# Time-mixing values kept once by token, the second direction read from them backwards, and a second raw-weight buffer in the first stage

## The chip, the cores and the metric

The kernel runs on one core of a Trainium2 chip. The metric is device time in microseconds (us) of one execution; the figure to compare is the median of several runs.

## The reference

One layer of a bidirectional hybrid backbone over 1024 latent tokens and 256 context tokens, 1024 channels, batch 1. A normalised and modulated input is projected by one matrix `w_in` into an S5 input, the RWKV-7 inputs (r, k, v and three low-rank columns) and gates. The two branches run side by side, are gated and merged, and a convolutional feed-forward follows. What matters here is the RWKV branch. It runs a delta rule over the tokens in both directions, 16 heads of 64 channels:

```python
def step(s, inp):
    rt, wt, kt, vt, at, bt = inp
    sa = jnp.einsum('bhvk,bhk->bhv', s, at)
    s = s * wt[:, :, None, :] + sa[..., None] * bt[:, :, None, :] + vt[..., None] * kt[:, :, None, :]
    return s, jnp.einsum('bhvk,bhk->bhv', s, rt)
...
ys_c, s_ctx = wkv7_scan(*ins_c, s_zero, rev)
ys_l, _ = wkv7_scan(*ins_l, s_ctx, rev)
```

Direction 1 reads the context tokens backwards and then the latent tokens backwards. The values v are the same for both directions.

## The kernel before

The program has three stages. **Stage A** (`stage_a`, from L600) normalises the input and runs the projections. Each projection job is a `dense` (L197): 8 x 3 matmuls a chunk of up to 512 tokens, since every weight is split into a high and a low part. `load_w` (L184) makes the two parts in two halves of 512 columns: SP issues the DMA of one half into the tile `wraw` (L191), ACT casts it to `whi` (L192), DVE subtracts to get `wlo` (L193). `wraw` has `E.nraw` buffers, and `E.nraw` is 1 through stage A (L1817) and 2 from stage C (L1858); `whi` and `wlo` have two buffers each. Around the projections the S5 branch runs in the same stage (`s5_in`, `s5_scan`, `s5_out`, lines 435 to 564), much of it on DVE and ACT; its loads (`s5bb`, `s5U`, `s5M`, `s5cc`) go through SP as well. The order in which the jobs of stage A are interleaved on the engines and on the queues is found by the framework's scheduler when the program is built, so jobs of the loop at L676 run between pieces of the S5 loop.

The loop at L676 has eight rounds j, one for each pair of heads (128 channels). It projects k, then v (`rw_job(16 + j)`, L678), then r. The v result `xs` is [128 channels, 1280 tokens]. It is stored as it is (L680), and also transposed: ten 128x128 transposes on TensorE into `pvt` (L687), three evictions by ACT into `vt` [128 tokens, 10, 128 channels] (L688), one store by POOL into the DRAM tensor `vT_d[j, 0]` by token (L689). Then SP issues two copies from DRAM to DRAM (L690 to L692): the rows of the 256 context tokens, and those of the 1024 latent tokens, each turned around, into `vT_d[j, 1]`. Both copies have the pattern "h t c": 2 heads outermost, then the tokens, then 64 channels (256 bytes) in one piece.

**Stage B** (`stage_b`, L1527) is the RWKV recurrence in 20 chunks of 64 tokens for each j, with both directions side by side, interleaved with the gate and GLU projections as filler work (`filler_nodes`). All of it is written as nodes of a `Plan` (L741). A node has an engine, a cost and dependencies; `order` (L761) is a list scheduler that puts all nodes into one order by due time, and PE, ACT and DVE run in that order. SP nodes ("s") cost 0.5 each in it. `chain_nodes` (L1160) holds the recurrence. Its helper `values` (L1173) loads the values of four chunks, both directions, into one of three tiles `V` [128, 2 directions, 4 chunks, 64]. Partitions 0 to 63 get the second head of the pair and 64 to 127 the first, through `OWN[1 - e]` at L1181. There are four loads, one for each direction and head, each of 256 tokens x 64 channels (64 KB) with the 64 tokens of a chunk on the partitions and outermost in the pattern. `values` is called five times for each j, 40 times in all, one block ahead of its use (L1215). The loads wait for the tile's earlier users (`gate`), and `B.a[d]` makes the chain wait for them.

**Stage C** (`stage_c`, L1647) has the output projections and the feed-forward. The change does not touch it.

SP issues its DMAs in order. The SP queue carries all weight loads, the S5 loads, the copies at L692, and in stage B the loads of every stage-B node.

Of the kernel before, what the change touches and what calls it, by code (L numbers as in the profile page):

```python
# [12 lines left out]
AF = mybir.ActivationFunctionType  # L13
# [6 lines left out]
CTX = 256  # L20
LAT = 1024
T = CTX + LAT
# [577 lines left out]
def stage_a(E):  # L600
    nc = E.nc
    with ExitStack() as st:
        spc = pool(E, st, "s5c", side="right")
        s_k = ExitStack()
        wp = stage_norm(E, st, spc, pool(E, s_k, "s5kc", side="right"))
        ps = E.ps
        rhs = lambda k, t0, n: (E.hh[:, k, t0:t0 + n], E.hl[:, k, t0:t0 + n])

        def u_load(U, g0):
            nc.sync.dma_start(U, E.u_d[g0 // 8, :, g0 % 8:g0 % 8 + 4, :])  # L610
        E.u_load = u_load

        def u_job(i):
            ut = wp.tile([128, 8, 160], FT, tag="raw", name="ut")

            def evac(pt, t0, n):
                nc.scalar.activation(ut[:, :, t0 // 8:(t0 + n) // 8], pt.rearrange("p (c s) -> p s c", s=8), AF.Copy)
            dense(E, wp, ps, E.I["win"][i], rhs, CH_ALL, evac, first=E.first if i == 0 else None)
            for g in range(8):
                nc.gpsimd.dma_start(E.u_d[i, :, g, :].rearrange("(s c) n -> c s n", c=16), ut[16 * g:16 * g + 16])  # L620

        def rw_job(m, chunks):
            raw = wp.tile([128, T], FT, tag="raw", name="raw")
            xs = wp.tile([128, T], FT, tag="xs", name="xs")

            def evac(pt, t0, n):
                nc.scalar.activation(raw[:, t0:t0 + n], pt, AF.Copy)
                nc.scalar.activation(xs[:, t0:t0 + n], pt, AF.Copy, scale=E.omu[:, m:m + 1])  # L628
            dense(E, wp, ps, E.I["win"][8 + m], rhs, chunks, evac)
            shift_lerp(E, m, raw, xs, chunks is CH_LAT)  # L630
            return xs

        def k_job(j):
            xs = rw_job(8 + j, CH_ALL)
            nc.gpsimd.dma_start(E.k_d[j], xs)
            kk = wp.tile([128, T], FT, tag="raw", name="kk")
            pk = ps.tile([128, 512], FT, tag="pz", name="pkk")
            for t0 in (0, 640):
                sq = kk[:, t0:t0 + 640]
                nc.scalar.activation(sq, xs[:, t0:t0 + 640], AF.Square, scale=E.par("kk", j))  # L640
                head_sums(E, pk[:, t0 // 64:], sq, 5)
            w = [wp.tile([128, 20], FT, tag=f"rs{i}", name=f"rs{i}", bufs=1) for i in range(3)]
            for f in rsqrt_small(E, w, lambda: pk[:, 0:20], None, None, 1e-24):
                f()

            def finish():
                for t0, n in CH_ALL:
                    pb = ps.tile([128, 512], FT, tag="pz", name="pkr")
                    head_spread(E, pb, w[1][:, t0 // 64:], n // 128)
                    nc.vector.scalar_tensor_tensor(kk[:, t0:t0 + n], xs[:, t0:t0 + n], E.par("kk", j), pb[:, :n],  # L650
                                                   op0=OP.mult, op1=OP.mult)
                nc.gpsimd.dma_start(E.kk_d[j], kk)
            return finish

        u_job(0)
        u_job(1)
        with ExitStack() as st2:
            s5_kernels(E, pool(E, st2, "s5k", 2, side="right"), ps)
        s_k.close()
        sp = pool(E, st, "s5p", side="right")  # L660
        S = s5_in(E, sp, ps, 0)
        for q in range(4):
            if q < 3:
                u_job(2 * q + 2)
                u_job(2 * q + 3)
                nxt = s5_in(E, sp, ps, q + 1)
            s5_scan(E, sp, S, q)
            s5_out(E, sp, ps, S, q)
            S = nxt
        xs = rw_job(24, CH_ALL)  # L670
        nc.scalar.activation(xs[0:64], xs[0:64], AF.Tanh)
        nc.gpsimd.dma_start(E.wda_d, xs)
        xs = rw_job(25, CH_LAT)
        nc.scalar.activation(xs[:, CTX:], xs[:, CTX:], AF.Sigmoid)
        nc.gpsimd.dma_start(E.gd_d, xs[:, CTX:])
        for j in range(8):  # L676
            finish = k_job(j)
            xs = rw_job(16 + j, CH_ALL)  # L678
            finish()
            nc.gpsimd.dma_start(E.v_d[j], xs)  # L680

            vt = wp.tile([128, 10, 128], FT, tag="raw", name="vt")
            for i in range(0, 10, 4):
                pv = ps.tile([128, 4, 128], FT, tag="pz", name="pvt")
                m = min(4, 10 - i)
                for q in range(m):
                    nc.tensor.transpose(pv[:, q, :], xs[:, 128 * (i + q):128 * (i + q) + 128], E.ident)  # L687
                nc.scalar.activation(vt[:, i:i + m], pv[:, 0:m], AF.Copy)  # L688
            nc.gpsimd.dma_start(E.vT_d[j, 0].rearrange("(i t) c -> t i c", t=128), vt)  # L689
            for c in (slice(0, CTX), slice(CTX, T)):  # L690
                src, dst = (E.vT_d[j, d, c].rearrange("t (h c) -> h t c", h=2) for d in range(2))
                nc.sync.dma_start(dst, src[:, ::-1])  # L692
            xs = rw_job(j, CH_LAT)
            nc.gpsimd.dma_start(E.r_d[j], xs[:, CTX:])

# [13 lines left out]
OWN = (slice(0, 64), slice(64, 128))  # L709
# [450 lines left out]
def chain_nodes(E, g):  # L1160


    nc, pl, j = E.nc, E.plan, g.j
# [7 lines left out]
    HALF = (0, 1)  # L1171

    def values(c0):  # L1173

        B, t0 = g.B[c0], 64 * c0
        sl, gate = E.V.next()
        B.V, B.Vslot = sl.tile, sl
        for d in HALF:
            for e in HALF:
                src = E.vT_d[j, d, t0:t0 + 256, 64 * e:64 * e + 64].rearrange("(i t) c -> t i c", t=64)  # L1180
                n = pl.add("s", 0.5, [gate], lambda d=d, e=e, src=src: nc.sync.dma_start(sl.tile[OWN[1 - e], d], src))  # L1181
                B.a[d].append(n)
                sl.users.append(n)

    def own(out, d, w, x, **kw):

# [621 lines left out]
def body(tc, I, O):  # L1808
    E = Env()
    E.tc, E.nc, E.I, E.O = tc, tc.nc, I, O  # L1810
    nc = tc.nc
    def ps_alloc(nb=None):
        E.ps = PsumPool(E, nb or {"d": 4})
    def ps_free():
        E.ps.st.close()
    E.ps_alloc, E.ps_free = ps_alloc, ps_free
    E.nraw = 1  # L1817
    with ExitStack() as st:
        E.const = pool(E, st, "const")
        E.dram = pool(E, st, "dram", 1, MS.DRAM)  # L1820
        dt = lambda n, s: E.dram.tile(s, FT, name=n, tag=n)
        E.u_d = dt("u_d", [8, 128, 8, 160])
        E.ge_d = dt("ge_d", [8, 128, LAT])
        E.r_d = dt("r_d", [8, 128, LAT])
        E.k_d = dt("k_d", [8, 128, T])
        E.kk_d = dt("kk_d", [8, 128, T])
        E.v_d = dt("v_d", [8, 128, T])
        E.sg_d = dt("sg_d", [16, 128, LAT])
        E.yg_d = dt("yg_d", [8, 128, LAT])
        E.y_d = dt("y_d", [8, 2, 128, LAT])  # L1830
        E.gd_d = dt("gd_d", [128, LAT])
        E.bon_d = dt("bon_d", [8, 2, 128, LAT])
        E.wda_d = dt("wda_d", [128, T])
        E.xn_d = dt("xn_d", [8, 128, LAT])
        E.vT_d = dt("vT_d", [8, 2, T, 128])
        E.inv_d = [[dt(f"{n}{k}", [64, 32, 32]) for n in ("LD", "TD", "AD")] for k in range(3)]
        E.acc_d = dt("acc_d", [8, 128, LAT])
        E.hx_d = dt("hx_d", [8, 128, LAT])
        constants(E)
        with ExitStack() as st1:  # L1840
            ps_alloc(NB_B)
            E.dtag = "sc"
            stage_a(E)
            with ExitStack() as st0:
                zero = pool(E, st0, "zero").tile([64, 256], FT, name="zero")
                nc.gpsimd.memset(zero, 0.0)
                for x in E.inv_d:
                    for q in x[1:]:
                        nc.gpsimd.dma_start(q.rearrange("l (a s) t -> l a (s t)", a=4),
                                            zero[:, None, :].to_broadcast([64, 4, 256]))  # L1850
            E.banks = [E.ps.tile([128, 512], FT, tag=n, name=f"bank{i}") for i, n in enumerate(
                ("ch", "ch", "ch", "z", "Y", "pz", "sc", "sc"))]
            keep = E.ps
            stage_b(E)
            E.ps = keep
            ps_free()
        E.dtag = "d"
        E.nraw = 2  # L1858
        ps_alloc({"d": 5, "s": 2})
        stage_c(E)  # L1860
        ps_free()
# [52 lines left out]
```

## Time and profile before

| what | us |
|---|---|
| median of 3 runs | 3232.58 |
| lowest and highest of the 3 | 3212.47 and 3235.23 |
| profiled execution, own time | 3210.84 |
| its span, first to last instruction | 3209.1 |
| TensorE busy in the span | 2861.5 |

The rows that follow come from the profiled execution. A line of a timeline has the start, the duration, engine, source line, operation, output<-input, the count, and in brackets the idle time of the engine before it and what ended it. PE is TensorE, DVE VectorE, ACT ScalarE, POOL GpSimd, SP the engine that issues most DMAs. For "SPq" a duration is the time that the issue of the DMA took, not the transfer.

### The profile page before, as it was taken

To read this page: it belongs to the slowest core of one execution; us is meant where nothing else is said; L and a number is where in the kernel's file an instruction comes from. 1 tells how busy PE (TensorE), PEld (TensorE's weight loads), DVE (VectorE), ACT (ScalarE), POOL (GpSimd) and SP (SyncE) were. 2 spreads that over 40 slices of the span, in tenths; PEclk is the share of its full clock that TensorE was granted. 3 is DMA by queue.
4 is the path that set the end of the run, shared out by engine and by line. 5 is a ranking of instruction groups with operands and counts; after the bars stand their busy time and mean duration, and the time that the engine had idled before them with its cause. 6 is when DMAs were issued, how large, how long until landed. Compare 5 with 4: busy or idle time off the path is not lost.

```text
span 3209.1 us, 83846 instructions
## 1 busy us (share of the span) xinstructions
PE 2861.5 (89%) x34806; PEld 2171.2 (68%) x34806; DVE 1837.2 (57%) x4640; ACT 1371.4 (43%) x3055; POOL 471.6 (15%) x781
## 2 busy tenths in 40 slices
PE   6999887878759999899888888898998999999998
PEld 2777676767536656666666666666875888887876
DVE  8758776772255546667585767745625434434343
ACT  6224544535234545555454555532215333333332
POOL 0430101011121313223132222201000000000000
PEclk8999898988878988989898998989998999999999
DMA  6763433434465556555555556545531111113332
GB/s 229 200 152 100 142 99 110 143 107 135 126 163 135 156 144 180 132 131 140 135 148 130 132 140 152 138 120 164 170 125 53 47 46 48 51 47 118 105 112 73
DMA packets 556878, 399.32 MB, mean 124 GB/s; under 512 B 374224, under 2 KB 460496, under 8 KB 555216
## 3 DMA queue, kind: packets, MB, share of 16 engines
q1 hardware_dynamic: 517824, 300.96, 33.9%
q0 software_dynamic: 29312, 87.75, 8.3%
q10 hardware_dynamic: 9360, 5.25, 0.8%
q8 instruction: 273, 4.47, 0.6%
q14 instruction: 109, 0.89, 0.1%
HBM read 286.16 MB, written 112.85 MB: 124 GB/s over the span
## 4 chain that ended last, share of the span: by engine, by line
PE 60%; DMA 11%; DVE 11%; issue 7%; ACT 6%; SPq 3%; POOL 1%; ACTq 0%; DVEq 0%; POOLq 0%
PE pd L206 8%; PE pd L208 8%; PE pd L207 8%; PE bank L1468 4%; DMA wraw<-win 3%; PE o L1755 3%; PE o L1756 3%; PE o L1757 3%; PE bank L1470 2%; PE bank L1469 2%; PE bank L1193 2%; PE bank L1188 2%; PE bank L1334 1%; PE bank L998 1%; DVE PR L1077 1%
## 5 line engine op out<-in xcount | busy, mean ns | idle before, releaser
L193 DVE TENSOR_TENSOR wlo<-wraw,whi 128x512 fp32r<-128x512 f32 x276 | 184.3, 689 | 500.3 <-ACT whi L192 499.5
L192 ACT ACTIVATE whi<-wraw 128x512 fp32r<-128x512 f32 x276 | 166.1, 627 | 547.8 <-PE pd L207 259.1
L206 PE MATMUL pd<-hh,whi 128*128 128x512 f32 (+1 forms) x744 | 287.9, 387 | 64.9 <-ACT xs L628 45.4
L206 PE MATMUL pd<-h2h,whi 128*128 128x512 f32 x704 | 275.6, 392 | 12.1 <-ACT h2h L1643 12.1
L207 PE MATMUL pd<-hl,whi 128*128 128x512 f32 (+1 forms) x744 | 283.8, 381 | 0.0
L208 PE MATMUL pd<-hh,wlo 128*128 128x512 f32 (+1 forms) x744 | 283.8, 382 | 0.0
L1468 PE MATMUL bank<-fxh,fwh 128*128 128x512 f32 x512 | 268.6, 525 | 17.1 <-ACT fo L1491 8.9
L208 PE MATMUL pd<-h2h,wlo 128*128 128x512 f32 x704 | 278.5, 396 | 0.0
L207 PE MATMUL pd<-h2l,whi 128*128 128x512 f32 x704 | 277.8, 395 | 0.6 <-DVE h2l L1644 0.5
L1470 PE MATMUL bank<-fxh,fwl 128*128 128x512 f32 x512 | 214.0, 418 | 0.9 <-issue 0.9
L1469 PE MATMUL bank<-fxl,fwh 128*128 128x512 f32 x512 | 213.9, 418 | 0.0
L206 PEld LDWEIGHTS pd<-hh,whi 128*128 128x128 f32 x744 | 150.3, 202 | 93.8 <-ACT xs L628 48.6
L208 PEld LDWEIGHTS pd<-hh,wlo 128*128 128x128 f32 x744 | 149.3, 201 | 26.0 <-issue 3.6
L207 PEld LDWEIGHTS pd<-hl,whi 128*128 128x128 f32 x744 | 150.1, 202 | 23.5 <-issue 1.9
L206 PEld LDWEIGHTS pd<-h2h,whi 128*128 128x128 f32 x704 | 133.0, 189 | 44.9 <-ACT h2h L1643 15.3
L207 PEld LDWEIGHTS pd<-h2l,whi 128*128 128x128 f32 x704 | 133.1, 189 | 33.2 <-DVE h2l L1644 2.2
L208 PEld LDWEIGHTS pd<-h2h,wlo 128*128 128x128 f32 x704 | 133.3, 189 | 26.5
L1468 PEld LDWEIGHTS bank<-fxh,fwh 128*128 128x128 f32 x512 | 101.9, 199 | 64.0 <-issue 20.6
L1448 DVE SCALAR_TENSOR_TENSOR fwl<-fr,fwh 128x512 fp32r<-128x512 f32 x128 | 95.2, 745 | 82.6 <-ACT fwh L1447 82.4
L1755 PE MATMUL o<-ph,whi 128*128 128x512 f32 x352 | 137.1, 394 | 2.2 <-ACT p L1729 2.2
L1756 PE MATMUL o<-pl,whi 128*128 128x512 f32 x352 | 138.1, 392 | 0.0
L1077 DVE TENSOR_TENSOR PR<-TN,LN 128x1 f32<-128x1 f32 (+9 forms) x360 | 117.3, 326 | 35.3 <-DMA LN<-LD 31.1
(395 smaller groups left out, 7132.6 us busy)
## 6 DMA issues: line engine op xcount, KB each, us to landing
wraw<-up SPq DMA_DIRECT2D x88, 256.0 KB
wraw<-down SPq DMA_DIRECT2D x88, 256.0 KB
wraw<-win SPq DMA_DIRECT2D x68, 256.0 KB
fin<-wmod SPq DMA_DIRECT2D x32, 512.0 KB
fr<-win SPq DMA_DIRECT2D x64, 256.0 KB
fr<-glu SPq DMA_DIRECT2D x64, 256.0 KB
s5U<-u_d SPq DMA_DIRECT2D x32, 320.0 KB
kk<-kk_d SPq DMA_DIRECT2D x80, 128.0 KB
```

Of the source, the lines that this page charges most:

```text
L192: nc.scalar.activation(hi[:, c], raw, AF.Copy)
L193: nc.vector.tensor_sub(lo[:, c], raw, hi[:, c])
L206: nc.tensor.matmul(pt[:, :n], hi[:, c], xh, start=k == 0, stop=False)
L207: nc.tensor.matmul(pt[:, :n], hi[:, c], xl, start=False, stop=False)
L208: nc.tensor.matmul(pt[:, :n], lo[:, c], xh, start=False, stop=k == 7)
L1077: last = [op("v", 0.07 + k * k / 960.0, last, lambda lo=lo, hi=hi, k=k, s=s: nc.vector.tensor_tensor(out=PR[al, :k * k].rearrange("l (c m) ...
L1468: nc.tensor.matmul(o, hi[:, c], xh[:, k, :], start=k == 0, stop=False)
L1469: nc.tensor.matmul(o, hi[:, c], xl[:, k, :], start=False, stop=False)
L1470: nc.tensor.matmul(o, lo[:, c], xh[:, k, :], start=False, stop=k == 7)
L1755: nc.tensor.matmul(o, hi[:, c], ph, start=k == 0, stop=False)
L1756: nc.tensor.matmul(o, hi[:, c], pl, start=False, stop=False)
L1757: nc.tensor.matmul(o, lo[:, c], ph, start=False, stop=k == 21)
```

## The change

The evictions of the transposed values write the two heads in swapped order, so that `vT_d` holds each token's row as (second head, first head). It is stored once, without a direction axis, and the two copies at L690 to L692 are gone. `values` now makes six loads: two for direction 0, one a head, as before with the partitions now in the stored order; and four for direction 1, one a chunk, each reading 64 token rows backwards for both heads into all 128 partitions (32 KB). `E.nraw` is 2 in stage A too.

```diff
@@ stage_a
-                nc.scalar.activation(vt[:, i:i + m], pv[:, 0:m], AF.Copy)
-            nc.gpsimd.dma_start(E.vT_d[j, 0].rearrange("(i t) c -> t i c", t=128), vt)
-            for c in (slice(0, CTX), slice(CTX, T)):
-                src, dst = (E.vT_d[j, d, c].rearrange("t (h c) -> h t c", h=2) for d in range(2))
-                nc.sync.dma_start(dst, src[:, ::-1])
+                by_head = lambda x: x.rearrange("p i (h c) -> p i h c", h=2)
+                nc.scalar.activation(by_head(vt[:, i:i + m])[:, :, ::-1], by_head(pv[:, 0:m]), AF.Copy)
+            nc.gpsimd.dma_start(E.vT_d[j].rearrange("(i t) c -> t i c", t=128), vt)
@@ chain_nodes, values
-        for d in HALF:
-            for e in HALF:
-                src = E.vT_d[j, d, t0:t0 + 256, 64 * e:64 * e + 64].rearrange("(i t) c -> t i c", t=64)
-                n = pl.add("s", 0.5, [gate], lambda d=d, e=e, src=src: nc.sync.dma_start(sl.tile[OWN[1 - e], d], src))
-                B.a[d].append(n)
-                sl.users.append(n)
+        r0 = 0 if t0 < CTX else CTX + T - t0 - 256
+        rows = E.vT_d[j, r0:r0 + 256][::-1].rearrange("t (h c) -> h t c", h=2)
+        parts = [(sl.tile[OWN[e], 0], E.vT_d[j, t0:t0 + 256, 64 * e:64 * e + 64].rearrange("(i t) c -> t i c", t=64))
+                 for e in HALF] + [(sl.tile[:, 1, i], rows[:, 64 * i:64 * i + 64]) for i in range(4)]
+        for k, (dst, src) in enumerate(parts):
+            n = pl.add("s", 0.5, [gate], lambda dst=dst, src=src: nc.sync.dma_start(dst, src))
+            B.a[int(k > 1)].append(n)
+            sl.users.append(n)
@@ body
-    E.nraw = 1
+    E.nraw = 2
-        E.vT_d = dt("vT_d", [8, 2, T, 128])
+        E.vT_d = dt("vT_d", [8, T, 128])
```

## Rows read from the trace of the kernel before

**Rows 1.** The page: busy time of the engines, and the chain that ended last

```profile
PE 2861.5 (89%) x34806; PEld 2171.2 (68%) x34806; DVE 1837.2 (57%) x4640; ACT 1371.4 (43%) x3055; POOL 471.6 (15%) x781
...
PE 60%; DMA 11%; DVE 11%; issue 7%; ACT 6%; SPq 3%; POOL 1%; ACTq 0%; DVEq 0%; POOLq 0%
```

**Rows 2.** Windows: length, busy PE, PEld, DVE, ACT, POOL, granted clock, DMA, GB/s

```profile
300.00:870.00 570.00, 466.81 (x2924) 389.08 (x2922) 350.90 (x760) 242.29 (x401) 74.19 (x124) 0.87 0.38 119
870.00:920.00 50.00, 13.02 (x158) 7.99 (x158) 14.60 (x27) 15.25 (x35) 7.24 (x11) 0.54 0.59 168
920.00:2230.00 1310.00, 1179.26 (x25764) 834.05 (x25763) 831.99 (x2732) 651.22 (x1837) 319.50 (x509) 0.92 0.55 142
```

**Rows 3.** Timeline of the SP queue, 747 to 770 us

```profile
747.36 0.58 SPq L692 DMA_DIRECT2D vT_d<-vT_d  x1
748.04 3.88 SPq L529 DMA_DIRECT2D s5M<-s5cd  x1
751.98 0.57 SPq L692 DMA_DIRECT2D vT_d<-vT_d  x1
754.32 14.98 SPq L191 DMA_DIRECT2D wraw<-win  x1
```

**Rows 4.** DMA view, 514 to 531 us: rate in 40 slices, the SP queue's share

```profile
GB/s 373 422 428 251 146 210 150 123 40 37 36 36 36 75 42 45 43 33 37 36 36 36 36 36 36 36 36 37 37 36 36 36 36 36 36 36 36 37 37 36
...
q1 hardware_dynamic: 1966, 0.50, 13.0%
```

**Rows 5.** Timelines: the SP issue and the ACT cast behind the third copy

```profile
513.70 17.70 SPq L191 DMA_DIRECT2D wraw<-win  x1
...
533.93 0.63 ACT L192 ACTIVATE whi<-wraw 128x512 fp32r<-128x512 f32 x1 [17.30 <-DMA wraw<-win]
```

**Rows 6.** Timeline of PE: the eight idle times that follow copies

```profile
355.67 4.43 PE L173 MATMUL pkk<-bones,kk 128*128 128x2 f32 x20 [3.17 <-ACT kk L640]
...
430.38 0.69 PE L451 MATMUL s5pb<-ident,s5tr 128*128 128x128 f32 x2 [10.90 <-DVE s5tr L299]
...
540.99 0.79 PE L206 MATMUL pd<-hh,whi 128*128 128x512 f32 x1 [14.97 <-ACT xs L628]
...
598.91 0.77 PE L547 MATMUL s5py<-s5U,s5M 128*128 128x128 f32 x2 [8.34 <-DMA s5U<-u_d]
...
755.35 0.80 PE L547 MATMUL s5py<-s5U,s5M 128*128 128x128 f32 x2 [4.00 <-DMA s5M<-s5cd]
...
776.64 0.58 PE L206 MATMUL pd<-hh,whi 128*128 128x256 f32 x1 [5.14 <-ACT xs L628]
...
843.89 0.58 PE L206 MATMUL pd<-hh,whi 128*128 128x256 f32 x1 [9.68 <-ACT xs L628]
...
906.95 1.03 PE L1379 MATMUL bank<-fin,cond 128*2 128x256 f32 x8 [15.08 <-DMA fin<-wmod]
```

**Rows 7.** Windows of 50 us in stage A, columns as in rows 2

```profile
450.00:500.00 50.00, 48.13 (x359) 40.18 (x358) 39.57 (x67) 32.74 (x51) 4.09 (x7) 1.00 0.49 161
500.00:550.00 50.00, 32.66 (x181) 28.24 (x180) 29.30 (x87) 16.40 (x28) 9.30 (x15) 0.80 0.31 92
```

**Rows 8.** Timelines: a weight load with no copy ahead, and PE behind it

```profile
392.47 4.66 SPq L191 DMA_DIRECT2D wraw<-win  x2
...
401.53 0.80 PE L206 MATMUL pd<-hh,whi 128*128 128x512 f32 x1 [6.51 <-ACT xs L628]
```

**Rows 9.** The value loads: all of them (ns: min/median/max), and one call's

```profile
L1181 SPq DMA_DIRECT2D V<-vT_d x160: 573/587/1866, 797.7 to 2133.6; - x160
...
1397.19 2.62 SPq L1181 DMA_DIRECT2D V<-vT_d  x4
```

**Rows 10.** Waits in stage B, 900 to 2230 us: total, times, longest

```profile
PE bank L1379 <- DMA fin<-wmod: 19.7, 3, 15.1
PE bank L1113 <- DMA AT<-AD: 8.8, 15, 3.6
...
SPq L940 <- DMA bon_d<-r: 48.2, 26, 6.0
```

**Rows 11.** ACT groups, 60 to 900 us: `vt` and, written with a stride, `ut`

```profile
L688 ACT ACTIVATE vt<-pvt 128x512 f32<-128x512 f32 x16 | 9.5, 597 | 10.6 <-PE pvt L687 10.3
...
L617 ACT ACTIVATE ut<-pd 128x512 f32<-128x512 f32 x16 | 9.4, 595 | 24.3 <-PE pd L208 8.8 <-DMA s5cd<-s5KA 6.6 <-DVE s5tr L299 4.1
```

## The prediction

> **What bounds the kernel now.** I read the page first: PE is busy 89% of the span, and the chain that ended last is PE for 60%, DMA for 11% [rows 1]. PE is thus the engine to look at, and the question is where it stands still. The windows by stage come next. From 920 to 2230 us PE is busy 1179 of 1310 us; from 300 to 870 us, where the loop over the values runs, only 467 of 570 at a granted clock of 0.87; and the 50 us between the stages hold 13 us of PE work [rows 2]. So the second half of stage A and the seam to stage B have some 140 us of idle PE in them. DVE is busy 351 of those 570 us and ACT 242, so neither is full.
>
> Then the SP queue around a copy. The sixth pair shows it best, since other DMAs stand between and behind its two copies [rows 3]. The context copy (128 KB) is issued in 0.58 us, but the next DMA's issue takes 3.88 us; the latent copy (512 KB) is issued in 0.57 us, and the weight load behind it takes 14.98 us. During a copy the DMA view shows a flat 36 GB/s, and the SP queue takes 13.0% of 16 engines' time, about two engines' worth [rows 4]. At 36 GB/s 128 KB take 3.6 us and 512 KB take 14.6 us. That is the issue time of the DMA behind, both times: SP's next issue ends when the copy before it has drained. Each pair of copies therefore closes SP for about 18 us, eight times, whatever is queued there.
>
> Last, what PE makes of it. Behind the third copy the weight load takes 17.70 us to issue, ACT stands 17.30 us at the cast of that weight [rows 5], and PE stands 14.97 us [rows 6]: the ACT eviction that the row names, which frees PE's accumulator, is queued on ACT behind that cast. The PE timeline has eight such idle times directly behind copies: 3.2, 10.9, 15.0, 8.3, 4.0, 5.1, 9.7 and, at the start of stage B where the last pair holds up the `wmod` load, 15.1 us [rows 6]. Their sum is 71.3 us. The fifth pair (at 661 us) leaves none, the sixth leaves two.
>
> **The copies go.** 71.3 us of idle PE lose their cause; the eight also lose what the clock does after them: the stretch without a copy ran at 1.00, the one with the 15 us hole at 0.80 [rows 7], that is, partly at the lower of 2.4 and 1.2 GHz. What is late next, once the weights are there, is ACT's and DVE's in-order work, part of which was queued up behind the same waits; DVE at 62% of the stage has room for most of it, not all. I take 55 of the 71.3 us. For the clock: 467 us of PE work at 0.87 would at 0.90 be 467 x (1 - 0.87/0.90) = 15.6 us shorter; I take 10. Bounds: 0 to 71 and 0 to 16.
>
> **Two raw buffers.** With one buffer a second half's DMA waits for the subtraction of the first. With no copy in the way, such a load (from the first half's issue to the end of the second's 4.66 us) still left PE idle for 6.5 us [rows 8]. With two buffers the halves load side by side and the weights are ready up to about 4 us sooner. There are a handful of such holes: 8 us taken, 0 to 20 as bounds. It adds no instruction.
>
> **The evictions** write the heads swapped. `ut` is written with a stride and takes 595 ns, `vt` without takes 597 [rows 11]: nothing taken. If the swapped form cost half as much again, 24 evictions would cost ACT 24 x 0.3 = 7 us over 570, hidden in its 58% of free time.
>
> **The loads of direction 1.** Here the change adds work. Before, a call of `values` is four issues of 64 KB in 2.62 us, the median issue 0.587 us [rows 9]. After, two of these stay and four of 32 KB with two heads outermost and the rows backwards come in the place of the other two. The trace of before has no such load; it bounds it from both sides. If they drain as quickly as the forward loads, each costs an issue: four times 0.59 in place of two, +1.2 us of SP a call, 40 calls, 47 us of SP time (below that there is no reason to go, since two issues more are made of the same bytes and the same pieces of 256 bytes). If they drain like the copies, whose pattern (two heads, then rows backwards, 256 bytes a piece) they share, 32 KB at 36 GB/s is 0.91 us, and each following issue waits for that: 4 x 0.91 = 3.64 in place of 2 x 0.59 = 1.17, +2.5 us a call, 40 calls, 99 us of SP. The copies are the nearer row, and I take +2.5 us.
>
> A page speaks to this. The Trainium skill, "DMA: Bandwidth & Descriptors", section "Why a DMA increments its semaphore by 16 and not by 1", says that a DMA is spread over at most as many engines as divide the slowest dimension of both sides, so a pattern that begins with 2 runs on two engines. The copies' 13.0% of 16 agrees with it [rows 4], and by that rule the new loads, which begin with the two heads on the DRAM side, run on two engines as well, which supports the higher price; without the rule one could hope that the 128 partitions of the destination spread them.
>
> How much of this reaches PE? Queued behind the value loads on SP are loads of the preparation (kk, k, r), the inverse's small DRAM round trips and the filler's weights. SP has slack: it waits 48.2 us in stage B for `bon_d` stores alone before it may refill a buffer [rows 10], so it runs ahead of its users there. But the inverse's round trips are waited for at once (8.8 us of PE in 15 waits already [rows 10]). Value loads themselves come a block ahead and are late for nobody. If a third of the 40 delays of 2.5 us hits such a chain, 33 us arrive there, and PE has filler to do for part of them: I take 20 us, with 0 and 40 x 3.64 = 146 us (all four drains, nothing hidden) as ends. Two more SP nodes a call also change the planner's order a little; that can go either way by some us.
>
> **The sum**, against the profiled 3210.84 us (span 3209.1, 1.7 outside): -55 - 10 - 8 + 20 = -53, to 3158. That execution was 22 us below the median shown, 3232.58; from the median the same step leads to 3180.
>
> **The rivals.** *The slow loads eat it.* Direction 1's loads close SP for 3.64 us each call and two DMA engines with it, and the preparation and the inverse stand behind them 33 us after 33 us: 146 us on the path against 73 won, 3232.6 + 73 = 3306. It decides from 1.8 us a call reaching PE (73/40). For it: SP issues in order and the copies show that a drain blocks it. Against: PE in stage B waits little for DMAs today [rows 10], so there is room. *The holes close elsewhere.* The S5 work on DVE and ACT shifts up against PE, and only the hole at the seam (15) and a third of the others (19) are won, no clock, against 30 lost in stage B: 3229, no change. For it: the rows behind several holes name DVE and ACT [rows 6]; against: they stood still through the same copies [rows 5]. *Everything is won.* The loads spread like the forward ones and hide, 71 + 16 + 8 = 95 us come back: 3138. Against it stands the copies' rate [rows 4].
>
> **How the numbers follow.** About 1% is what a measurement of this kernel can tell from no change: 3200 to 3265. The forecast, 3180 with 3155 to 3208 of its own, gets 0.48; everything won 0.19; the holes close elsewhere 0.24; the slow loads eat it 0.09. The range must leave out little more than the last: 3130 to 3242. Faster is 0.43 of the forecast's 0.48, all of everything won and 0.02 of the second rival: 0.64; slower the first rival, 0.09; the rest, 0.27, is no change.
>
> **What would show it.** No copy rows; the longest issue of a weight load in stage A falls from 17.7 us to under 3. The window from 300 to 870 us keeps its PE work but ends some 60 us sooner, at a clock near 0.90, and the seam has no 15 us wait for `wmod`. A call of `values` takes about 4 to 5 us of SP in place of 2.6, with a flat low DMA rate during it. Wrong would be: holes of the old size before the same matmuls with other releasers (second rival), stage B longer than before by more than 70 us (first), or value loads of under 3 us a call (third).

## The result and the profile after

The changed kernel takes 3123.56 us (median of 4 runs, 3109.12 to 3133.19) where the kernel before takes 3233.9 (4 runs, 3212.47 to 3267.71). The ratio is 0.9669, with a 95% interval of 0.9614 to 0.9724: 3.3% faster, some 107 us. The prediction was 3180 in a range of 3130 to 3242, so the sign was right, the gain was twice the forecast, and the median lies 6 us below the range. The case it came to is the third rival, "everything is won", with a bit more on top. The profiled executions of the two kernels are the fastest of each, and differ by 102 us.

The page of the changed kernel, busy time of the engines and the chain that ended last, against [rows 1]:

```profile
span 3107.3 us, 84016 instructions
PE 2849.6 (92%) x34806; PEld 2172.2 (70%) x34806; DVE 1837.0 (59%) x4640; ACT 1373.9 (44%) x3055; POOL 473.6 (15%) x781
...
PE 67%; issue 11%; DVE 8%; DMA 6%; ACT 5%; POOL 1%; SPq 1%; ACTq 0%; DVEq 0%; POOLq 0%
```

The engines do the same work in 102 us less. DMA falls from 11% to 6% of the chain, SP's queue from 3% to 1%.

Where the time went shows by two marks: the last projection matmul of stage A (L208 on `hh`), and the first matmul of stage C (L206 on `ygh`). The groups of PE for the tile `pd` have them as first and last start, here of the kernel before and then of the changed one (ns: min/median/max of one matmul):

```profile
L208 PE MATMUL pd<-hh,wlo x744: 274/389/774, 70.0 to 862.7; 128*128 128x512 f32 x136, 128*128 128x256 f32 x50
...
L206 PE MATMUL pd<-ygh,whi x128: 393/396/796, 2238.5 to 2329.8; 128*128 128x512 f32 x128
```

```profile
L208 PE MATMUL pd<-hh,wlo x744: 277/389/776, 68.2 to 767.6; 128*128 128x512 f32 x136, 128*128 128x256 f32 x50
...
L206 PE MATMUL pd<-ygh,whi x128: 393/396/796, 2135.3 to 2226.3; 128*128 128x512 f32 x128
```

Call the first "mark A". Stage A ends 95.1 us sooner, stage B from there takes 1367.7 in place of 1375.8 us, and stage C 972.0 in place of 970.6. Nearly everything is won in stage A. The windows up to mark A (columns as in [rows 2]), before:

```profile
0.00:300.00 300.00, 259.91 (x1947) 192.91 (x1948) 222.15 (x517) 119.07 (x229) 65.89 (x129) 0.94 0.58 177
300.00:862.70 562.70, 460.64 (x2788) 384.75 (x2786) 350.00 (x758) 239.19 (x394) 67.62 (x114) 0.87 0.37 118
```

and after:

```profile
0.00:300.00 300.00, 267.63 (x2029) 202.69 (x2030) 229.67 (x548) 121.74 (x235) 66.45 (x130) 0.96 0.59 182
300.00:767.60 467.60, 428.66 (x2694) 358.52 (x2692) 336.40 (x713) 234.32 (x382) 63.19 (x105) 0.94 0.39 126
```

PE was idle for 862.7 - 720.6 = 142.1 us and is now idle for 767.6 - 696.3 = 71.3. That is 71 us (that it equals the prediction's sum of holes is chance). Its busy time for nearly the same matmuls (4735 and 4723) falls from 720.6 to 696.3, another 24 us: the granted clock rose from 0.87 to 0.94, more of the stage at 2.4 GHz and less at 1.2. 71 + 24 are the 95. Each edit also changes the order that the scheduler finds for stage A; what that alone is worth in a mark, no run here separates.

What ended ACT's wait before the casts of the weights (L192), in the same stretch from 300 us, before:

```profile
  DMA wraw<-win: 112.3, 20
  PE pd L207: 32.2, 9
```

and after:

```profile
  PE pd L207: 27.6, 10
```

The 112.3 us in which ACT stood for a weight DMA are gone altogether, and with them the holes of [rows 6] in stage A: 3.4 us are the longest that is left between 320 and 700 us. The longest issue of a weight load there falls from 17.7 to 1.9 us. At the seam to stage B the 15 us wait for `wmod` is gone too (the longest is 4.2 us now). This is stage B in two windows, its first 50 us and the rest, before and after:

```profile
862.70:912.70 50.00, 14.40 (x230) 8.78 (x228) 13.31 (x26) 14.83 (x33) 13.09 (x19) 0.61 0.62 177
912.70:2238.50 1325.80, 1186.16 (x25837) 839.00 (x25837) 837.79 (x2743) 657.55 (x1850) 320.77 (x511) 0.91 0.56 143
```

```profile
767.60:817.60 50.00, 30.43 (x408) 20.13 (x408) 29.18 (x67) 26.88 (x60) 22.05 (x37) 0.66 0.80 225
817.60:2135.30 1317.70, 1180.85 (x25676) 842.86 (x25670) 827.53 (x2717) 650.55 (x1828) 317.65 (x502) 0.90 0.56 142
```

PE's idle time in stage B falls from 175.2 to 156.4 us, most of it in the first 50. Its busy time rises from 1200.6 to 1211.3, so that 8 of these 19 us are left.

The value loads look as the prediction had them at one place only. These are three calls, issued in one train when stage A is about to end (SP timeline); the DMA rate during it; and then all 240 loads (ns: min/median/max) and three of them in stage B:

```profile
721.96 14.88 SPq L1182 DMA_DIRECT2D V<-vT_d  x18
```

```profile
GB/s 410 339 377 366 366 344 292 213 244 401 408 223 209 46 40 33 36 36 35 46 101 116 139 81 15 36 36 36 36 36 80 36 163 71 169 40 11 36 36 36
...
L1182 SPq DMA_DIRECT2D V<-vT_d x240: 484/533/2884, 722.0 to 2027.6; - x120
...
1000.91 1.94 SPq L1182 DMA_DIRECT2D V<-vT_d  x3
```

The train takes 14.88/3 = 4.96 us a call, and stretches of it run at the copies' flat 36 GB/s. That agrees with the rule that the prediction quotes from the Trainium skill ("DMA: Bandwidth & Descriptors", section "Why a DMA increments its semaphore by 16 and not by 1"): the two-head loads run on about two engines although their destination has 128 partitions. How much of the 14.88 us is due to that, e5 below shows. Later the loads stand between other loads: of the 148 two-head ones outside the train 107 stand alone, and of the three loads at 1000.91 us only one is two-head (32 KB). Most single issues then take 0.5 to 0.65 us, and no drain shows in most of the issues behind them. Added up over the SP timeline, all value loads take 150 us of SP, 3.75 a call, where they took 118 before, 2.95 a call.

### The profile page after: what moved, and what is told of

Its sections match the earlier page's. It is cut to its first block, busy times and chain, and to the rows that moved or that the text cites. A ratio compares the mean times of both kernels' runs of the same rounds, so it can differ in the third digit from the quotient of the medians.

```text
span 3107.3 us, 84016 instructions
## 1 busy us (share of the span) xinstructions
PE 2849.6 (92%) x34806; PEld 2172.2 (70%) x34806; DVE 1837.0 (59%) x4640; ACT 1373.9 (44%) x3055; POOL 473.6 (15%) x781
## 4 chain that ended last, share of the span: by engine, by line
PE 67%; issue 11%; DVE 8%; DMA 6%; ACT 5%; POOL 1%; SPq 1%; ACTq 0%; DVEq 0%; POOLq 0%
PE pd L206 10%; PE pd L208 10%; PE pd L207 10%; PE bank L1469 5%; PE bank L1194 3%; PE bank L1471 3%; PE bank L1470 3%; PE o L1756 3%; PE o L1757 3%; PE o L1758 3%; PE bank L1189 3%; PE bank L1335 1%; PE bank L949 1%; DVE PR L1075 1%; PE bank L996 1%
## 5 line engine op out<-in xcount | busy, mean ns | idle before, releaser
L192 ACT ACTIVATE whi<-wraw 128x512 fp32r<-128x512 f32 x276 | 161.8, 625 | 383.8 <-PE pd L207 256.5
L206 PE MATMUL pd<-hh,whi 128*128 128x512 f32 (+1 forms) x744 | 281.3, 378 | 25.0 <-ACT xs L628 11.4
L206 PE MATMUL pd<-h2h,whi 128*128 128x512 f32 x704 | 279.7, 398 | 12.0 <-ACT h2h L1644 12.0
L208 PE MATMUL pd<-h2h,wlo 128*128 128x512 f32 x704 | 277.6, 395 | 0.0
L208 PE MATMUL pd<-hh,wlo 128*128 128x512 f32 (+1 forms) x744 | 277.3, 373 | 0.0
L206 PEld LDWEIGHTS pd<-hh,whi 128*128 128x128 f32 x744 | 145.5, 196 | 52.0 <-ACT xs L628 13.1
L206 PEld LDWEIGHTS pd<-h2h,whi 128*128 128x128 f32 x704 | 133.6, 190 | 41.7 <-ACT h2h L1644 15.3
L208 PEld LDWEIGHTS pd<-hh,wlo 128*128 128x128 f32 x744 | 144.8, 195 | 22.6 <-issue 0.8
L208 PEld LDWEIGHTS pd<-h2h,wlo 128*128 128x128 f32 x704 | 133.2, 189 | 30.8
L1758 PE MATMUL o<-ph,wlo 128*128 128x512 f32 x352 | 136.3, 392 | 0.0
```

The costliest lines, as they stand in the source:

```text
L192: nc.scalar.activation(hi[:, c], raw, AF.Copy)
L206: nc.tensor.matmul(pt[:, :n], hi[:, c], xh, start=k == 0, stop=False)
L208: nc.tensor.matmul(pt[:, :n], lo[:, c], xh, start=False, stop=k == 7)
L1758: nc.tensor.matmul(o, lo[:, c], ph, start=False, stop=k == 21)
```

## The experiments

Three questions: which of the two edits made the gain in stage A, why two edits that were priced separately overlap, and what the new loads cost. Each ratio is to the kernel before, measured beside the run on the same chip; its medians there lie between 3225.8 and 3232.4. Runs from different chips are compared by their ratios. Marks and idle times are worked out as above, from each run's profile. The profile of e3 is of its slowest execution (3221.8 us, its fastest took 3174.7), so e3's mark may be late.

| run | copies | raw buffers | mark A, us | PE idle up to it | median, us | ratio (95%) |
|---|---|---|---|---|---|---|
| before | on SP | 1 | 862.7 | 142 | 3233.9 | |
| e1 | none | 1 | 783.9 | 82 | 3121.8 | 0.9668 (0.962 to 0.9717) |
| e2 | on SP | 2 | 800.1 | 98 | 3178.5 | 0.9834 (0.979 to 0.9879) |
| changed | none | 2 | 767.6 | 71 | 3123.6 | 0.9669 (0.9614 to 0.9724) |
| e3 | on POOL | 1 | 822.8 | 113 | 3196.1 | 0.9895 (0.9858 to 0.9932) |
| e7 | on POOL | 2 | 797.0 | 101 | 3168.6 | 0.9827 (0.9774 to 0.9879) |

**e1, the changed kernel with one raw buffer.**

```diff
-    E.nraw = 2
+    E.nraw = 1
```

> The changed kernel with one raw-weight buffer in stage A: the copies are gone, the second buffer is not there. Before, the last projection matmul of stage A starts at 862.7 us, after the change at 767.6, 95 us sooner; I had counted some 53 for the copies with their clock and 8 for the buffers. Theory 1, the copies close the SP queue and that is nearly all: 3130 to 3150, stage A's last projection matmul at 775 to 795. Rival, the second buffer gives a third or more, since it lets weights run ahead of every stall of the queue: 3160 or later, that matmul at 800 or later.

Measured: 3121.8 us, the changed kernel's time. Mark A comes at 783.9, 79 us before that of the kernel before and 16 after that of the changed one. Theory 1 holds; without the copies the second buffer is worth at most those 16 us in stage A, and none of it shows in the whole time.

**e2, the kernel before with two raw buffers.**

```diff
-    E.nraw = 1
+    E.nraw = 2
```

> The kernel before with two raw-weight buffers in stage A, the copies left in. Theory 1: some 10 to 20 us faster than before, about 3215, since the second buffer does not open a queue that a copy holds shut. Rival, the buffer is a large part: 30 us or more faster, 3200 or below. If both edits work on the same stalls, the two gains alone add up to more than the 110 us of both; if each needs the other, to less.

Measured: 52 us faster, mark A 63 us sooner. Here the rival was right and theory 1 wrong: alone, the buffer is a large edit. The two gains alone, 63 and 79 us of stage A, add up to 141, and both edits together give 95. They remove the same holes. What ended ACT's waits before the weight casts in stage A says it, e1 first and then e2:

```profile
  PE pd L207: 26.0, 13
  DMA wraw<-win: 24.0, 13
```

```profile
  PE pd L207: 21.2, 10
  DMA wraw<-win: 14.7, 2
```

From 112.3 us either edit leaves little of the wait for weights. In e1 SP is open when the load is due: the longest issue of a weight load in stage A is 0.7 us. In e2 it is still 17.3 us, so the copies close SP as before; that ACT hardly waits must then come from weights loaded ahead of the copy, which the second buffer allows. What two weight buffers can't cover are the other loads behind a copy. This is e2 at the seam, where the last copies stand ahead of loads of stage B, on SP and then on PE:

```profile
825.45 14.35 SPq L940 DMA_DIRECT2D r<-r_d  x1
...
846.54 0.48 PE L998 MATMUL bank<-Q,BK 64*64 64x64 f32 x4 [21.99 <-DVE BK L977]
```

**e3 and e7, the kernel before with its copies on POOL**, in five pieces of 128 KB, with one raw buffer and with two.

```diff
-            for c in (slice(0, CTX), slice(CTX, T)):
-                src, dst = (E.vT_d[j, d, c].rearrange("t (h c) -> h t c", h=2) for d in range(2))
-                nc.sync.dma_start(dst, src[:, ::-1])
+            for a, b in [(0, 0)] + [(CTX + 256 * m, T - 256 - 256 * m) for m in range(4)]:
+                src, dst = (E.vT_d[j, d, c:c + 256].rearrange("t (h c) -> h t c", h=2) for d, c in ((0, a), (1, b)))
+                nc.gpsimd.dma_start(dst, src[:, ::-1])
```

> The kernel before with its copies issued by POOL in place of SP, the latent rows in four pieces of 256 tokens, one raw buffer, values loaded as before. The same bytes move in the same pattern, but SP is never held. Theory 1, the harm is SP's issue held shut: most of the gain in stage A comes though the copies stay, stage A's last projection matmul at 780 to 810, whole time 3140 to 3180. Rival, the harm is the transfer itself (two engines held, later loads sharing them) or POOL's own stores queued behind the copies: that matmul at 840 or later, 3200 or above.

> The kernel before with its copies on POOL in five pieces and with two raw-weight buffers. With one buffer it was 3196, the last projection matmul of stage A at 823 us, ACT's waits for weights still 74 us. If what is left there is weight loads that land late beside the copies' traffic, the second buffer covers them: that matmul at 785 to 800, 3150 to 3170. If it is POOL's own queue (stores of the S5 part and of k and kk behind the copies), the buffer helps little: 3185 or more.

Measured: e3 is 34 us faster than before, mark A at 822.8; between the two expectations. The holes of 10 and 15 us are gone from its stage A, so the closed SP queue did make those, but it has many of 3 to 7 us left. Its waits in stage A, and under them those of e7 (waiting instruction <- releaser: total, times, longest):

```profile
ACT whi L192 <- DMA wraw<-win: 74.4, 18, 9.7
ACT s5y L555 <- DMA ge_d<-s5y: 25.4, 6, 7.4
```

```profile
ACT s5y L555 <- DMA ge_d<-s5y: 42.7, 8, 16.2
POOL vT_d L692 <- DMA vT_d<-vt: 21.5, 6, 6.1
```

In e3 ACT still waits 74.4 us for weights, where e1 without copies waits 24.0. The longest landing of a weight load is 7.8 us, with a median of 2.7; that the copies' traffic makes it late is argued, not shown. The second buffer of e7 takes these waits away, mark A goes to 797 and the time to 3168.6, as the first branch expected. Against the changed kernel POOL's queue is left: the S5 part's stores stand behind the copies, and ACT waits 42.7 us for the buffers that they free, where it waits 13.8 in the changed kernel. So the copies harm through whichever queue they are on. With one raw buffer they harm more on SP: on POOL the kernel is 1% faster. With two there is no difference that can be measured: e2 and e7 have ratios of 0.9834 and 0.9827, and marks of 800.1 and 797.0. Nowhere were they free.

**e4, e5 and e6, the loads and the plan.** e4 reads direction 1 forwards in two loads a call, e5 forwards in four, and e6 keeps the backward loads but puts two in one planner node. In e4 and e5 direction 1 takes its values in the wrong order inside a block; they are there for the time alone. The main lines that differ, of e5 and of e6:

```diff
-                 for e in HALF] + [(sl.tile[:, 1, i], rows[:, 64 * i:64 * i + 64]) for i in range(4)]
+                 for e in HALF] + [(sl.tile[OWN[e], 1, 2 * q:2 * q + 2], E.vT_d[
+                     j, r0 + 128 * q:r0 + 128 * q + 128, 64 * e:64 * e + 64].rearrange("(i t) c -> t i c", t=64))
+                     for q in HALF for e in HALF]
```

```diff
-        for k, (dst, src) in enumerate(parts):
-            n = pl.add("s", 0.5, [gate], lambda dst=dst, src=src: nc.sync.dma_start(dst, src))
+        for k, some in enumerate((parts[0:1], parts[1:2], parts[2:4], parts[4:6])):
+            def load(some=some):
+                for dst, src in some:
+                    nc.sync.dma_start(dst, src)
+            n = pl.add("s", 0.5, [gate], load)
```

> The changed kernel with direction 1's value loads replaced by two loads of 64 KB that read the same rows forwards, one a head with the tokens outermost (so direction 1 takes its values in the wrong order inside a block of 256 tokens). It takes the two-head pattern and two issues a call away. If the backward loads cost stage B the 20 us of the prediction: 3100 to 3107, stage B shorter by 15 to 25 us. If the planner's order hides them, the same as the changed kernel within 6 us, 3118 to 3130.

> The changed kernel with the same six loads a call in the planner, but direction 1's four read forwards, 64 tokens outermost, one head and two chunks each (32 KB; direction 1 takes its values in the wrong order). Only the two-head backward pattern is taken away; the planner's nodes are those of the changed kernel. If that pattern costs stage B anything, this is faster than the changed kernel's 3124 by it: 3104 with the 20 us of the prediction. If the pattern is hidden, 3117 to 3130. The run with forward loads in two pieces came out slower (3145), with other planner nodes; if the order of the plan is what made that, this one stays near 3124, and if forward loads as such are slower, near 3145.

> The changed kernel with its four backward loads in two planner nodes, two loads a node, so that the planner has as many nodes as before the change. If the plan's order makes the 20 us between the changed kernel (3124) and the run with two forward pieces (3145), this is near 3145. If the pattern costs something when two loads stand back to back, it is slower still, 3155 or more. If neither matters, 3117 to 3130.

Measured: e4 3145.3 us (ratio 0.9717, 0.9651 to 0.9782), e5 3126.5 (0.9687, 0.9641 to 0.9733), e6 3144.2 (0.9725, 0.9672 to 0.9777). e5 equals the changed kernel, so against forward loads of the same number and size the two-head backward pattern costs nothing that these runs can measure. The intervals are some 16 us to each side, so a cost of a few us is not excluded, and the forecast 20 us only just is. Even the train at the end of stage A owes little to the pattern. The same 18 loads at the same place, all forwards, take in e5:

```profile
727.07 12.52 SPq L1183 DMA_DIRECT2D V<-vT_d  x18
```

Of the changed kernel's 14.88 us the pattern thus accounts for 2.4, 0.8 a call. Over the whole timeline e5's value loads take even more of SP, 175 us against 150.

e4 and e6 have four planner nodes a call, and both come out 20 us later. e6 has the changed kernel's loads, so there it is the order, not the loads. It does not come from loads that stand closer together: in e6, too, where two share a node, 98 of the 148 two-head loads outside the train stand alone. One thing that the two orders differ in is how long PE waits in stage B for the inverse's round trips, here of e6 and then of the changed kernel:

```profile
PE bank L1111 <- DMA AT<-AD: 15.8, 12, 5.2
```

```profile
PE bank L1111 <- DMA AT<-AD: 4.0, 6, 2.0
```

**e9, e10 and e11, is it the number of nodes?** e9 is the kernel before with six nodes a call (direction 1's two loads split into four), e10 the changed kernel with eight, e11 the changed kernel once more. The main lines of e10:

```diff
-        parts = [(sl.tile[OWN[e], 0], E.vT_d[j, t0:t0 + 256, 64 * e:64 * e + 64].rearrange("(i t) c -> t i c", t=64))
-                 for e in HALF] + [(sl.tile[:, 1, i], rows[:, 64 * i:64 * i + 64]) for i in range(4)]
+        parts = [(sl.tile[OWN[e], 0, 2 * q:2 * q + 2], E.vT_d[j, t0 + 128 * q:t0 + 128 * q + 128, 64 * e:64 * e + 64].rearrange(
+            "(i t) c -> t i c", t=64)) for q in HALF for e in HALF] + [(sl.tile[:, 1, i], rows[:, 64 * i:64 * i + 64]) for i in range(4)]
```

> The kernel before, copies and one raw buffer kept, with direction 1's two value loads of a call split into four of 32 KB by chunk pairs, so that the planner has the six nodes of the changed kernel. Two pairs of runs (3124 and 3126 with six nodes, 3144 and 3145 with four) point to 20 us that come from the planner's order alone. If that holds apart from the copies: 3205 to 3215 against 3228 of before, stage A as before. If the 20 us need the change, or the pairs fell so by chance: 3220 to 3240.

> The changed kernel with direction 0's two value loads split into four as well, eight nodes a call. If more, smaller loads as such make the plan better (SP's time in the plan nearer to what SP needs), 3105 to 3120. If the 20 us are one order that happened to come out well, this lands anywhere between 3115 and 3150.

> The changed kernel once more, as a control on the same chip: 3115 to 3130. If it comes near 3144, the 20 us between plans were the chip or chance.

Measured: e9 3237.2 us (ratio 1.0015, 0.9989 to 1.0041), e10 3142.9 (0.9718, 0.9671 to 0.9765), e11 3124.6 (0.9673, 0.963 to 0.9716). Eight nodes are as late as four, and six give nothing in the kernel before. The 20 us, 0.6%, thus go with one order that came out well with the changed loads, and not with the number of nodes. The intervals of single pairs overlap; that three six-node runs without copies (3123.6, 3124.6, 3126.5) stand against three others (3142.9, 3144.2, 3145.3) is what carries it, and this grouping was made after they were seen.

What makes the 20 us stays open. The profiles do not show it as idle time: PE is idle in stage B for 156 us in the changed kernel, 160 in e11 and 166 in e5, and for 160 in e4, 155 in e6 and 164 in e10. The shorter waits for AT are thus made up by other waits. What differs more is PE's busy time for the same matmuls, and that differs between executions of one kernel as well: 1211 us in the changed kernel, 1231 in e11, 1236 in e6.

**e8 and e12, twice the loads.** Every backward load is followed in its node by one of the same size into a spare tile that nobody reads; in e8 with the two-head backward pattern, in e12 forwards with the tokens outermost. The main lines added in e8:

```diff
+            def load(dst=dst, src=src, k=k):
+                nc.sync.dma_start(dst, src)
+                if k > 1:
+                    nc.sync.dma_start(E.spare[:, k - 2], src)
```

> The changed kernel with each of direction 1's backward loads made twice, the second into a spare tile that nobody reads, in the same planner node: 160 loads of 32 KB more in the two-head pattern, the same plan. It doubles the suspected cost. If each two-head load closes SP for its 0.91 us and the wait reaches PE, some 40 times 3.6 = 146 us at most are added, and 20 us if only what the prediction took gets through: 3144. If SP's slack hides them, 3120 to 3132.

> The run with the doubled loads, but its 160 spare loads read forwards, 64 tokens outermost, one head and two chunks each: 32 KB each as there, same planner nodes, nobody reads them. In the run with two-head spares (3217, 94 us more than the changed kernel) they all stood together in the first 260 us of stage B. If the harm was the two-head pattern holding SP's queue, most of the 94 us go: 3135 to 3165. If 160 more issues at that place cost that much whatever their pattern: 3200 to 3230.

Measured: e8 3217.2 us (ratio 0.9972, 0.9936 to 1.0009), e12 3173.7 (0.9816, 0.9778 to 0.9853). e8 doesn't measure what it was made for: all spare loads, which no reader holds back, stand in one crowd at the head of stage B. The issues of the spares in e8 and in e12 (ns: min/median/max, first and last start):

```profile
L1185 SPq DMA_DIRECT2D spare<-vT_d x160: 484/810/4647, 726.2 to 989.1; - x160
```

```profile
L1186 SPq DMA_DIRECT2D spare<-vT_d x160: 573/602/2698, 727.6 to 947.2; - x160
```

Together they still give a price. In a crowd, 160 more loads cost some 50 us whatever their pattern (e12 against the changed kernel), and the two-head pattern another 44, 0.27 us a load. These are 200 us of stage B in e8, from 50 us behind mark A, PE busy 127 of 200 us, and the same stretch of the changed kernel, 183 of 200 (columns as in [rows 2]):

```profile
820.00:870.00 50.00, 22.62 (x288) 14.49 (x289) 18.13 (x47) 13.98 (x33) 8.22 (x12) 0.62 0.50 139
870.00:920.00 50.00, 36.68 (x606) 22.36 (x604) 24.19 (x63) 18.44 (x42) 14.52 (x22) 0.76 0.64 153
920.00:970.00 50.00, 30.58 (x384) 19.13 (x384) 14.74 (x46) 12.47 (x32) 3.20 (x4) 0.70 0.36 93
970.00:1020.00 50.00, 37.17 (x886) 25.36 (x886) 16.86 (x58) 17.57 (x48) 2.81 (x4) 0.82 0.64 139
```

```profile
818.00:868.00 50.00, 43.38 (x753) 27.52 (x757) 31.06 (x89) 22.57 (x52) 16.82 (x24) 0.85 0.75 187
868.00:918.00 50.00, 47.95 (x1003) 31.73 (x999) 25.36 (x80) 19.84 (x52) 3.82 (x4) 0.91 0.58 125
918.00:968.00 50.00, 48.85 (x1190) 34.65 (x1183) 25.97 (x69) 36.32 (x106) 16.24 (x27) 1.00 0.60 158
968.00:1018.00 50.00, 43.20 (x1013) 29.47 (x1013) 30.23 (x101) 20.82 (x59) 17.04 (x26) 0.93 0.65 170
```

What PE waits for most there are the `wmod` loads: 42.7 us in e8, 25.2 in e12 and 7.6 in the changed kernel.

No run beats the changed kernel by more than the noise; e1, without the second buffer, equals it.

## Why the prediction was right in kind and half in size

- *The copies close SP, and ACT and PE stand behind it.* Right, and shown by e1: taking the copies away alone gives the whole 3.3%, and ACT's wait for weights goes from 112.3 to 24.0 us.
- *The sum, -53 us.* This is where it failed: three of its terms had the wrong size. The profiled pair gained 102 us. Of the 49 us between, 19 are idle time of stage A, 14 are the clock, and 16 are stage B, where the loads were priced (stage C was 1.4 us longer, which the sum did not have).
- *"I take 55 of the 71.3 us."* The discount rested on ACT's and DVE's queued work, which was to be late next. It was not. Shared out by size, 43 of the 55 belong to stage A, and with the 8 of the second buffer 51; measured are 71. With only the copies taken away (e1) stage A loses 60 us of idle PE, where the seven holes counted there were 56, and the first 50 us of stage B hold 13 us more of PE work. So the list of holes was a low count by some us, not a ceiling to be cut down.
- *The clock, "I take 10", 0 to 16.* The granted clock was asked to rise from 0.87 to 0.90 and rose to 0.93 in e1 and 0.94 in the changed kernel: 19 and 24 us, above the bound.
- *"8 us taken, 0 to 20 as bounds" for the second buffer.* Right as an addition (16 us of stage A beyond e1, none of it in the whole time), wrong as a reading of what it does: alone it gives 52 us (e2), since it bridges the very holes that the copies make. The sum counted the two edits as separate; they share their cover.
- *The loads of direction 1, "+2.5 us a call" and 20 us.* The drain at 36 GB/s was right, the cost was not. SP spends 0.8 us more a call, below the prediction's lower bound of 1.2, and the 20 us did not appear (e5). The price was that of four loads in a row that each wait for the drain of the one ahead. Such rows were rare: the two-head loads mostly went out singly (107 of 148; 98 in e6, where they share planner nodes), and even the train of 18 took only 2.4 us more than forward loads.
- *Stage B as a whole.* Forecast: 11.6 us won at the seam (15.1 x 0.77) and 20 lost, +8; the profile shows -8. Its idle time fell by 19 us, the seam and a little more, and its busy time rose by 11. The order of the plan, named as going either way by some us, went with some 20 us of the medians (e6 and e10 against e11); no cause of it is shown.
- *The rivals.* "The slow loads eat it" fell with e5; "the holes close elsewhere" fell with the idle time of stage A. "Everything is won", 3138, had 0.19 and was the nearest. Its 95 us equal the 95 of stage A by chance: it took 15 of them from the seam and 16 from the clock, where stage A alone won 71 of idle time and 24 of clock.

## What to carry to other kernels

Two edits that remove the same wait must be priced together: a second buffer ahead of a blocked queue and the opening of that queue bought 63 and 79 us of stage A alone, 95 as a pair. When holes on the busiest engine all trace to one closed queue, and the engines named as next were themselves standing at that queue, there is little reason to discount them: here the full count, with the clock, was still too low. A DRAM pattern with a short outermost dimension cost nothing here as single small loads, 0.2 to 0.3 us a load in a train or a crowd, and some 18 us of a closed queue as a pair of long copies: look at what else is queued behind it.

## What the runs showed of the hardware

A copy whose pattern begins with two heads moves at 36 GB/s with 13.0% of the 16 engines' time [rows 4], and SP's next issue ends when it has drained: 3.88 us behind 128 KB, 14.98 us behind 512 KB [rows 3]. A 32 KB load of that pattern does not show it by itself: single ones were issued in 0.5 us. A train of eighteen value loads, twelve of them with that pattern, took 14.88 us, and eighteen forward loads of the same sizes 12.52 (e5). On POOL a 128 KB copy of the same pattern took 1.6 us to issue and 11.0 us in the median to land, here all copies of e3:

```profile
L692 POOL DMA_DIRECT2D vT_d<-vT_d x40: 1597/1607/1713, 326.6 to 855.8; - x40
...
vT_d<-vT_d POOLq DMA_DIRECT2D x40, 128.0 KB, 11.0
```

The same kernel's stage B differs between executions by more than some of the edits here: the changed kernel and its repeat (e11) took 1367.7 and 1391.5 us for it in their profiled runs. 20 of the 24 us between are busy time of PE, 1211.3 and 1231.2 us for the same work, at a granted clock of 0.89 and 0.88.
